# A two-layer transformer encoder: the feed-forward residual loaded in four groups across the output products, and the gate product in the norm's accumulator banks

## The chip, the cores and the metric

One core of one Trainium2 chip runs the whole program. The time is device microseconds (us) of one launch, from the runs' own timer. Engines: TensorE (PE: matmuls; PEld is its weight load), VectorE (DVE), ScalarE (ACT), GpSimd (POOL) and the queues that issue transfers (SPq for SyncE, ACTq for ScalarE). PSUM, the accumulator memory, has 8 banks of 128 x 512 fp32 numbers.

## The reference, cut to what matters

Two layers over 1024 tokens of width 1024. Each layer has a mixer (windowed attention in layer 0, a gated scan in layer 1), a norm, the feed-forward part, a norm, and a gated addition:

```python
x = layer_norm(ALPHA * x + mix, ln_mix_g[i], ln_mix_b[i])
x = layer_norm(ALPHA * x + swiglu(x, ffn_w_in[i], ffn_w_out[i]), ln_ffn_g[i], ln_ffn_b[i])
x = x + jax.nn.sigmoid(x @ ple_w_gate[i]) * (p[i] @ ple_w_proj[i])
```

The change touches the output product of `swiglu` (2816 to 1024), the `ALPHA * x` that is added to it (the residual), the second norm, and the last line's gate product `x @ ple_w_gate[i]`.

## The kernel before, in words

Activations lie transposed, as 8 tiles (128 features x 512 tokens) for each half of the tokens: `Y[m][h]`, m from 0 to 7, h 0 or 1. A product in fp32 is made of three matmuls (`mm3`, L342 to L345) on operands that `split` (L72 to L74) has taken apart into a high part (a copy on ACT) and a low part (a subtraction on DVE or POOL). One such matmul has 128 x 512 outputs.

Everything lives in pools of equal buffers. `A(...)` takes one of 49 SBUF buffers of 128 x 512 fp32 (pool "acts"): raw weights on their way in (`get`, L144 to L147, name `wraw`), the residual `Y`, and most intermediate tiles. `fx["pool"]` (`hp`) has 16 buffers for split operands. PSUM has two pools: `MM(...)` with 3 banks for the whole program, and in this part `bank(...)` with 5 banks (`fps`).

`ffn_ple(li, X, Y, pend)` (L699 to L959) is the feed-forward part of layer `li`; it runs once in each layer. Its stages are `matmuls_in` (22 hidden tiles, L805), `matmuls_out` (L827), and `ple` for each half of the tokens (L918). The output product is made in 7 passes, `ORDER = [1, 2, 6, 7, 4, 5, 3]`, each over 11 steps `k` (FP = 11). A step takes one pair of operands, a weight tile `wo` and a hidden tile `hs`, and adds it into four banks: 12 matmuls. Passes 1, 6, 7 and 4 sum into four banks `ox`, passes 2, 5 and 3 into `oz`, which is one `bank` and three `MM` banks (L877). At the end of a pass, `done(p, i)` (L837 to L863) adds the four results on DVE to four residual tiles: pass 1 uses `Y[0..3][0]` first, pass 6 `Y[0..3][1]`, pass 7 `Y[4..7][1]`, pass 4 `Y[4..7][0]`.

Pairs come through a plan. `take_w("o", p, k, ahead=6)` (L125) hands out the pair of step k, splits pairs until six more are ready, and begins the raw loads of two steps past the last pair split (L115 to L123). Each pair is two loads of 256 KB on SPq, one of `wfo` or its sums and one of the hidden tiles that were kept in memory. The residual is 16 loads of 256 KB on SPq (L834), written ahead of all passes.

When pass 4 is done, the norm of the first half (`norms[0]`) is woven into passes 5 and 3. After pass 3, `weave(ple(0), norms[1], 0.7)` (L954) makes the gate products of the first half (8 products `pgps`, 24 matmuls each) and beside them the norm of the second half: for each step of `ple(0)` (6 matmuls) it takes 0.7 steps of the norm. Products `pgps` are in `MM` banks; the norm's `mu` and `var` (L423, L444) are in `bank`. The gate is read by a sigmoid on ACT (L929), multiplied on DVE (L930) and added to `Y` on POOL (L931). The norm ends, tile by tile, in L452 (DVE), L453 and a copy `xh` (ACT) and `xl` (L74 on POOL); `ple(1)`, the gate products of the second half, reads those.

The kernel writes no order by hand across engines; the instructions of an engine or a queue stand in an order that the building framework makes from the program's order and the buffers that are free. Each engine and queue then works its list from front to end.

Of the kernel before, what the change touches and what calls it, by code (L numbers as in the profile page):

```python
# [17 lines left out]
KT = D // P  # L18
# [9 lines left out]
KH = KT // 2  # L28
# [5 lines left out]
def build(tc, xT, pT, wqkv, watt_o, whg, wvh, whg_o, wfi, wfo, wpg, wpp, sink, lbl, ngd, lnp,  # L34
          rope, amask, hmask, ident, outT):
    nc = tc.nc
    sync, act, dve, pool, pe = nc.sync, nc.scalar, nc.vector, nc.gpsimd, nc.tensor
# [8 lines left out]
    with (  # L46
# [16 lines left out]
        def A(name, dt=F32):  # L63
            return ap_.tile([P, HALF], dt, tag="a", name=name)

        def T(tag, name, bufs=2, dt=F32):
            return tp.tile([P, HALF], dt, tag=tag, bufs=bufs, name=name)

        def MM(name):
            return mp.tile([P, HALF], F32, tag="mm", name=name)  # L70
# [44 lines left out]
        def fetch_w():  # L115
            if at[0] < len(plan):
                while begun[0] < min(at[0] + 3, len(plan)) and (begun[0] <= at[0] or plan[begun[0]][3]):
                    if plan[begun[0]][3]:
                        plan[begun[0]][3]()
                    begun[0] += 1  # L120
                key, fn, args, _ = plan[at[0]]
                ready.append((key, fn(*args)))
                at[0] += 1  # L123

        def take_w(*key, ahead=1):  # L125
            if not ready:
                fetch_w()
            k, w = ready.pop(0)
            assert k == key, (k, key)
            while len(ready) < ahead and at[0] < len(plan) and (not ready or plan[at[0]][3]):  # L130
                fetch_w()
            return w

        fx = {}
# [216 lines left out]
        def lin_steps(w, xs, ps):  # L351
            for k, (wk, xk) in enumerate(zip(w, xs)):
                mm3(ps, wk, xk, k == 0, k == len(xs) - 1)
                if k % 2:
                    yield

        def lin(w, xs, name):
            ps = MM(name)
            yield from lin_steps(w, xs, ps)
            return ps  # L360

        def weave(main, side, ratio=1):
            due = 0.0
            for _ in main:
                due += ratio
                while due >= 1:
                    next(side, None)
                    due -= 1
            drain(side)

        def drain(gen):
            for _ in gen:
                pass
# [6 lines left out]
        def sum_in(s, y, m, yprev, eng=None):  # L380
            if m == 1:
                (eng or dve).tensor_tensor(s, yprev, y, op=ALU.add)
            elif m > 1:
                (dve if m == KT - 1 else eng or dve).tensor_tensor(s, s, y, op=ALU.add)
# [314 lines left out]
        def ffn_ple(li, X, Y, pend):  # L699
            with (  # L700
# [7 lines left out]
                xs = fx["x"] = {p: [] for p in (3, 4, 5, 6, 7)}  # L708
# [5 lines left out]
                def bank(name):  # L714
                    return fps.tile([P, HALF], F32, tag="f", name=name)
# [84 lines left out]
                def store(n=0):  # L800
                    while len(lag) > n:
                        for dst, src in lag.pop(0):
                            act.dma_start(dst, src)
# [22 lines left out]

                def matmuls_out():  # L827
                    s = {}
                    for m in range(KT):
                        for h in range(2):  # L830
                            Y[m][h] = A(f"y{m}{h}")
                    for m0, h in ((0, 0), (0, 1), (KH, 1), (KH, 0)):
                        for m in range(m0, m0 + KH):
                            sync.dma_start(Y[m][h], fx["y"][m, h])  # L834
                    xb, zb = [], []

                    def done(p, i):  # L837
                        x, z = xb[i] if xb else None, zb[i] if zb else None
                        if p == 1:
                            y = Y[i][0]  # L840
                            dve.scalar_tensor_tensor(y, y, ALPHA, x, ALU.mult, ALU.add)
                        elif p == 2:
                            y = Y[i][0]
                            dve.tensor_tensor(y, y, z, op=ALU.add)
                            sum_up(0, i)
                        elif p == 6:
                            y = Y[i][1]
                            dve.scalar_tensor_tensor(y, y, ALPHA, x, ALU.mult, ALU.add)
                        elif p == 7:
                            y = Y[KH + i][1]  # L850
                            dve.scalar_tensor_tensor(y, y, ALPHA, x, ALU.mult, ALU.add)
                        elif p == 4:
                            y = Y[KH + i][0]
                            dve.scalar_tensor_tensor(y, y, ALPHA, x, ALU.mult, ALU.add)
                            sum_up(0, KH + i)
                        elif p == 5:
                            y = Y[KH + i][1]
                            dve.tensor_tensor(y, y, z, op=ALU.add)
                            sum_up(1, KH + i)
                        else:  # L860
                            y = Y[i][1]
                            dve.tensor_tensor(y, y, z, op=ALU.add)
                            sum_up(1, i)  # L863

                    order = {0: list(range(KT)), 1: [*range(KH, KT), *range(KH)]}

                    def sum_up(h, m):
                        n = order[h].index(m)
                        if n == 0:
                            s[h] = T("to", f"s{h}")  # L870
                        sum_in(s[h], Y[m][h], n, Y[order[h][0]][h], pool)

                    for p in ORDER:
                        if p == 1:
                            xb[:] = [bank("ox") for _ in range(4)]
                        elif p in (2, 5):
                            zb[:] = [bank("oz"), *(MM("oz") for _ in range(3))]  # L877
                        into = xb if p in (1, 6, 7, 4) else zb
                        for k in range(FP):
                            if p == 1 and k == 1:  # L880
                                late.pop()()
                            if p == 1 and k == 4:
                                store()
                            w, hh = take_w("o", p, k, ahead=6)
                            for i in range(4):
                                mm3(into[i], w[i], hh, p in (1, 2, 5) and k == 0, k == FP - 1, True)
                                if k == FP - 1:
                                    done(p, i)
                            yield
                            yield  # L890
                        if p == 4:
                            xb.clear()
                            norms[0] = layer_norm([Y[m][0] for m in range(KT)], s[0], li, 1, X, 0, None, bank)
                            yield "half"
                    norms[1] = layer_norm([Y[m][1] for m in range(KT)], s[1], li, 1, X, 1, None, bank)
# [22 lines left out]
                def ple(h):  # L918
                    xs = [X[k][h] for k in range(KT)]
                    for m in range(KT):  # L920
                        pr = T("t1", "pr")
                        sync.dma_start(pr, fx["pr"][m, h])
                        ps = yield from lin(take_w("pg", m, ahead=2), xs, "pgps")
                        sg = T("t0", "psg")
                        end = li == 1 and m == KT - 1
                        w = HALF // 2 if end else HALF
                        for a in range(0, HALF, w):
                            c = slice(a, a + w)
                            act.activation(sg[:, c], ps[:, c], AF.Sigmoid)  # L929
                            dve.tensor_tensor(sg[:, c], sg[:, c], pr[:, c], op=ALU.mult)  # L930
                            (dve if end else pool).tensor_tensor(Y[m][h][:, c], Y[m][h][:, c], sg[:, c], op=ALU.add)  # L931
                            if li == 1:
                                sync.dma_start(outT[m * P:(m + 1) * P, h * HALF + a:h * HALF + a + w], Y[m][h][:, c])
# [6 lines left out]
                norms = {}  # L940
# [10 lines left out]
                while next(out) != "half":  # L951
                    pass
                weave(out, norms[0], 0.9)
                weave(ple(0), norms[1], 0.7)  # L954
                if li == 1:
                    drain(ple(1))
                    return None
# [324 lines left out]
        Y = [[None, None] for _ in range(KT)]  # L1282
# [94 lines left out]
```

## Time and profile before

| | |
|---|---|
| median of 3 runs | 2837.53 us (2830.99 to 2837.82) |
| the profiled execution's own time | 2838.45 us |
| its span, first to last instruction | 2836.7 us |
| mean granted TensorE clock | 0.98 of full speed |
| matmuls | 12852 |
| HBM read, written | 259.84 MB, 88.08 MB |

The span is what the views of the trace are measured in; all stretches are given from its start. A matmul's busy time overlaps the next one's, so that a busy PE is read by how many matmuls start in a stretch. The profile's clock share is 1.00 at 2.4 GHz and 0.50 at 1.2 GHz.

### The profile page before, as it was taken

The page shows a single profiled execution, that of the slowest core. Times are in us where ns is not written, and L with a number is a line of the kernel's source. Part 1 is how long each engine was busy: PE and PEld are TensorE (multiplying, and loading weights), DVE is VectorE, ACT ScalarE, POOL GpSimd, SP SyncE. Part 2 cuts the span into 40 slices and gives each one's busy share as a digit, 9 for nine tenths or more (in the row PEclk, how much of TensorE's full clock was granted, in tenths as well). Part 3 has the DMA queues.
Part 4 walks back from the last instruction along what each step waited for, and adds up shares of the span by engine and source line. Part 5 has one row for each costly group of instructions (what it writes and reads, how often), then busy time and mean ns, then how long its engine had stood idle before and what let it go on. Part 6 is the DMA issues. An engine that isn't in the chain of part 4 may idle for free.

```text
span 2836.7 us, 36978 instructions
## 1 busy us (share of the span) xinstructions
PE 2702.2 (95%) x12852; PEld 2182.9 (77%) x12852; DVE 1840.3 (65%) x2886; ACT 1267.7 (45%) x2482; POOL 1278.8 (45%) x904
## 2 busy tenths in 40 slices
PE   8999999899999899899999999999989999999999
PEld 6666676688888787687878878787667888878777
DVE  6787888755555557827656476667886555556685
ACT  4555667233333445634443344434562333344463
POOL 4233232665565747563222222221336556556563
PEclk9999999999999999999999999999999999999999
DMA  4111136454445952311011111113355444488243
GB/s 164 45 45 45 38 107 220 157 174 151 158 155 180 362 192 92 103 55 54 30 38 34 45 38 34 34 34 125 110 191 195 149 158 147 148 277 301 79 162 112
DMA packets 188827, 350.37 MB, mean 124 GB/s; under 512 B 21472, under 2 KB 24288, under 8 KB 188640
## 3 DMA queue, kind: packets, MB, share of 16 engines
q1 hardware_dynamic: 142560, 264.10, 28.0%
q10 hardware_dynamic: 46080, 83.91, 8.2%
q8 instruction: 101, 1.65, 0.2%
q14 instruction: 86, 0.70, 0.1%
HBM read 259.84 MB, written 88.08 MB: 123 GB/s over the span
## 4 chain that ended last, share of the span: by engine, by line
PE 38%; DVE 7%; POOL 4%; issue 4%; ACT 2%; DMA 1%; SPq 0%; ACTq 0%; POOLq 0%; DVEq 0%
PE zps L345 3%; PE zps L343 3%; PE zps L344 3%; PE lv L1109 3%; PE x L343 3%; PE x L345 3%; PE x L344 3%; POOL wo L74 2%; PE zy L343 1%; PE zy L345 1%; PE zy L344 1%; DVE Q L1079 1%; PE pgps L344 1%; PE pgps L345 1%; PE pgps L343 1%
## 5 line engine op out<-in xcount | busy, mean ns | idle before, releaser
L74 DVE TENSOR_TENSOR wp<-wraw,wp 128x512 fp32r<-128x512 f32 x200 | 212.4, 1063 | 163.2 <-ACT wp L73 135.8
L74 DVE TENSOR_TENSOR hs<-wraw,hs 128x512 fp32r<-128x512 f32 x154 | 208.4, 1371 | 141.9 <-ACT hs L73 139.9
L74 POOL TENSOR_TENSOR wo<-wraw,wo 128x512 fp32r<-128x512 f32 x154 | 225.8, 1479 | 156.8 <-ACT wo L73 155.7
L73 ACT CAST wp<-wraw 128x512 fp32r<-128x512 f32 x200 | 124.6, 623 | 294.1 <-PE x L345 149.5
L74 POOL TENSOR_TENSOR w_hz<-r_hz,w_hz 128x512 fp32r<-128x512 f32 x70 | 96.1, 1379 | 301.1 <-ACT w_hz L73 292.9
L343 PE MATMUL x<-xc,wp 128*128 128x512 f32 x528 | 211.2, 401 | 10.3 <-ACT u L728 7.2
L345 PE MATMUL x<-xc,wp 128*128 128x512 f32 x528 | 210.9, 399 | 0.0
L344 PE MATMUL x<-xc,wp 128*128 128x512 f32 x528 | 210.1, 398 | 0.0
L343 PE MATMUL zps<-xh_n,w_hz 128*128 128x512 f32 x512 | 209.9, 410 | 0.0
L345 PE MATMUL zps<-xh_n,w_hz 128*128 128x512 f32 x512 | 203.6, 398 | 0.9 <-POOL w_hz L74 0.9
L344 PE MATMUL zps<-xl_n,w_hz 128*128 128x512 f32 x512 | 202.8, 396 | 0.0
L73 ACT CAST wo<-wraw 128x512 fp32r<-128x512 f32 x154 | 95.4, 620 | 190.0 <-POOL wo L74 114.4
L343 PE MATMUL ox<-hs,wo 128*128 128x512 f32 x352 | 137.9, 395 | 11.4 <-ACT hs L73 11.4
L345 PE MATMUL ox<-hs,wo 128*128 128x512 f32 x352 | 139.1, 395 | 1.3 <-POOL wo L74 1.3
L344 PE MATMUL ox<-hs,wo 128*128 128x512 f32 x352 | 139.5, 396 | 0.4 <-DVE hs L74 0.3
L186 POOL TENSOR_TENSOR wraw<-s,wraw 128x512 f32<-128x512 f32 x34 | 45.1, 1325 | 202.5 <-DVE wp L74 201.7
L343 PEld LDWEIGHTS x<-xc,wp 128*128 128x128 f32 x528 | 100.0, 189 | 37.4 <-ACT u L728 8.1
L345 PEld LDWEIGHTS x<-xc,wp 128*128 128x128 f32 x528 | 100.0, 189 | 25.4 <-DVE wp L74 0.6
L344 PEld LDWEIGHTS x<-xc,wp 128*128 128x128 f32 x528 | 100.0, 189 | 23.5
L345 PEld LDWEIGHTS zps<-xh_n,w_hz 128*128 128x128 f32 x512 | 97.4, 190 | 21.4 <-POOL w_hz L74 1.3
L344 PEld LDWEIGHTS zps<-xl_n,w_hz 128*128 128x128 f32 x512 | 97.7, 191 | 16.7
L343 PEld LDWEIGHTS zps<-xh_n,w_hz 128*128 128x128 f32 x512 | 97.5, 190 | 16.3
(380 smaller groups left out, 8197.1 us busy)
## 6 DMA issues: line engine op xcount, KB each, us to landing
wraw<-in_wfi_dram SPq DMA_DIRECT2D x196, 256.0 KB, 3.2
wraw<-in_wfo_dram SPq DMA_DIRECT2D x154, 256.0 KB, 4.1
wraw<-h SPq DMA_DIRECT2D x154, 256.0 KB, 4.9
wraw<-w SPq DMA_DIRECT2D x88, 256.0 KB, 5.3
r_hz<-in_whg_dram SPq DMA_DIRECT2D x70, 256.0 KB, 2.8
w<-wraw ACTq DMA_DIRECT2D x66, 256.0 KB, 2.9
h<-th ACTq DMA_DIRECT2D x66, 256.0 KB, 2.1
r_pg<-in_wpg_dram SPq DMA_DIRECT2D x32, 512.0 KB, 4.2
```

The source lines that it names most:

```text
L73: act.copy(hi, src)
L74: (eng or dve).tensor_tensor(lo, src, f32(hi), op=ALU.subtract)
L186: pool.tensor_tensor(a11, tmp, a11, op=ALU.subtract)
L343: pe.matmul(ps, lhsT=w[0], rhs=x[0], start=start, stop=False, skip_group_check=free)
L344: pe.matmul(ps, lhsT=w[0], rhs=x[1], start=False, stop=False, skip_group_check=free)
L345: pe.matmul(ps, lhsT=w[1], rhs=x[0], start=False, stop=stop, skip_group_check=free)
L1079: dve.tensor_tensor(Qq[:, 1 - d], qk[:, 0], t["F"][:, d], op=ALU.mult)
L1109: pe.matmul(lv[:, c], lhsT=ks[:, c * P:(c + 1) * P], rhs=view(Qq, c * P, dims), start=True, stop=True)
```

## The change

`lin` takes a bank from its caller if one is given. The 16 residual loads are no longer written ahead of the passes, but in four groups of four, at steps k = 5 to 8 of passes 1, 2, 6 and 7: each ahead of that step's `take_w`, each with its own buffer taken at that point. The gate products take a `bank` in place of an `MM` bank, and the weave of the gate products with the second norm takes 0.85 steps of the norm for a step in place of 0.7.

```diff
-        def lin(w, xs, name):
-            ps = MM(name)
+        def lin(w, xs, name, ps=None):
+            ps = MM(name) if ps is None else ps
...
                 def matmuls_out():
                     s = {}
-                    for m in range(KT):
-                        for h in range(2):
-                            Y[m][h] = A(f"y{m}{h}")
-                    for m0, h in ((0, 0), (0, 1), (KH, 1), (KH, 0)):
-                        for m in range(m0, m0 + KH):
-                            sync.dma_start(Y[m][h], fx["y"][m, h])
+                    wanted = {p: [(m0 + i, h) for i in range(KH)]
+                              for p, m0, h in ((1, 0, 0), (2, 0, 1), (6, KH, 1), (7, KH, 0))}
...
                             if p == 1 and k == 4:
                                 store()
+                            if p in wanted and k >= 5 and wanted[p]:
+                                m, h = wanted[p].pop(0)
+                                Y[m][h] = A(f"y{m}{h}")
+                                sync.dma_start(Y[m][h], fx["y"][m, h])
                             w, hh = take_w("o", p, k, ahead=6)
...
-                        ps = yield from lin(take_w("pg", m, ahead=2), xs, "pgps")
+                        ps = yield from lin(take_w("pg", m, ahead=2), xs, "pgps", bank("pgps"))
...
-                weave(ple(0), norms[1], 0.7)
+                weave(ple(0), norms[1], 0.85)
```

## Rows read from the trace of the kernel before

**Rows 1.** The page: busy us (share of the span) x instructions, by engine.

```profile
PE 2702.2 (95%) x12852; PEld 2182.9 (77%) x12852; DVE 1840.3 (65%) x2886; ACT 1267.7 (45%) x2482; POOL 1278.8 (45%) x904
```

**Rows 2.** Waits of PE over the span: us in total, times, longest.

```profile
PE ox L343 <- ACT hs L73: 11.4, 2, 8.4
PE pgps L343 <- DVE y L862: 6.0, 2, 4.3
PE pgps L344 <- POOL xl L74: 4.4, 6, 1.1
```

**Rows 3.** Layer 0's pass 1 in stretches: PE, PEld, DVE, ACT, POOL busy (x); clock; DMA share, GB/s.

```profile
925.00:930.00 5.00, 0.76 (x4) 0.30 (x2) 0.00 (x0) 0.00 (x0) 0.00 (x0) 1.00 0.83 281
930.00:935.00 5.00, 0.80 (x2) 0.71 (x3) 0.82 (x1) 1.85 (x3) 1.45 (x2) 0.51 1.02 362
935.00:940.00 5.00, 5.00 (x13) 3.83 (x13) 1.22 (x2) 1.14 (x2) 4.92 (x4) 0.50 1.05 391
...
950.00:980.00 30.00, 30.00 (x134) 24.86 (x133) 25.60 (x21) 18.20 (x32) 24.77 (x17) 1.00 1.05 386
```

**Rows 4.** Timeline of SPq, layer 0, then layer 1: start, us, what.

```profile
901.58 0.33 SPq L79 DMA_DIRECT2D r_hv<-in_wvh_dram  x1
...
912.93 15.34 SPq L834 DMA_DIRECT2D y<-y  x16
928.37 0.38 SPq L146 DMA_DIRECT2D wraw<-in_wfo_dram  x1
...
2509.59 12.85 SPq L834 DMA_DIRECT2D y<-y  x16
```

**Rows 5.** Timeline of ACT, then POOL, layer 0's pass 1: [idle before <- releaser].

```profile
932.86 0.62 ACT L73 CAST wo<-wraw 128x512 fp32r<-128x512 f32 x1 [15.08 <-DMA wraw<-in_wfo_dram]
...
941.24 0.62 ACT L73 CAST hs<-wraw 128x512 fp32r<-128x512 f32 x1 [3.20 <-POOL th L789]
...
919.40 1.74 POOL L74 TENSOR_TENSOR w_hz<-r_hz,w_hz 128x512 fp32r<-128x512 f32 x1
```

**Rows 6.** Matmuls into `ox` in two stretches: us, PE busy (x), PEld, DVE, clock, DMA.

```profile
910.16:951.75 41.59, 32.52 (x128) 25.72 (x127) 1.07 (x2) 0.88 0.89 309
2511.16:2547.29 36.13, 32.05 (x128) 24.69 (x127) 0.67 (x1) 0.95 0.94 320
```

**Rows 7.** The page's DMA issues (median us to landing), and `done` of passes 7 and 4 by tile.

```profile
y<-y SPq DMA_DIRECT2D x32, 256.0 KB, 4.5
...
L851 DVE SCALAR_TENSOR_TENSOR y<-y,ox x8: 673/674/687, 1039.9 to 2638.4; 128x512 f32<-128x512 f32 x8
L854 DVE SCALAR_TENSOR_TENSOR y<-y,ox x8: 673/674/689, 1070.0 to 2668.5; 128x512 f32<-128x512 f32 x8
```

**Rows 8.** Timeline from pass 3 to `ple(0)`: PE in both layers, DVE and ACT in layer 0.

```profile
1142.59 0.77 PE L343 MATMUL pgps<-xh,w_pg 128*128 128x512 f32 x1 [4.33 <-DVE y L862]
...
2737.33 0.47 PE L343 MATMUL pgps<-xh,w_pg 128*128 128x512 f32 x1 [1.72 <-DVE y L862]
...
1147.11 0.68 DVE L384 TENSOR_TENSOR s<-s,y 128x512 f32<-128x512 f32 x1
...
1151.16 0.60 ACT L929 ACTIVATE psg<-pgps 128x512 f32<-128x512 f32 x1 [1.16 <-PE pgps L345]
1151.65 0.61 ACT L73 CAST avh<-s 128x512 fp32r<-128x512 f32 x1
```

**Rows 9.** Matmuls into `pgps` in stretches (PE, PEld, ACT); POOL at the end of the norm.

```profile
1142.59:1151.16 8.57, 8.57 (x25) 6.83 (x26) 0.00 (x1) 0.65 0.07 22
...
1195.00:1207.00 12.00, 9.42 (x27) 6.60 (x26) 0.60 (x1) 0.72 0.30 108
1207.00:1219.00 12.00, 12.00 (x53) 9.66 (x52) 1.20 (x2) 1.00 0.16 44
...
2787.00:2793.00 6.00, 4.20 (x16) 2.50 (x15) 0.00 (x0) 1.00 0.57 197
...
1195.45 5.07 POOL L74 TENSOR_TENSOR xl<-y,xh 128x512 fp32r<-128x512 f32 x3
```

## The prediction

> **What bounds the kernel now.** I read the page first: TensorE is busy 95% of the span, no other engine over 77% [rows 1]. So time is won only where TensorE stands still or runs at half clock. The waits of PE name three such places in this part of the program, once in each layer: the output product waits for a hidden tile's copy (11.4 us), the first gate product waits for the DVE instruction that reads the last `oz` (6.0), and the second half's gate products wait for `xl`, the norm's last tiles (4.4) [rows 2]. The idle time is not all of it, so I took stretches next. In layer 0, TensorE starts 2 matmuls from 930 to 935 us and 13 from 935 to 940, at a clock share of 0.51 and 0.50, that is 1.2 GHz, after five microseconds in which it was almost idle; from 950 to 980 it starts 134 at 2.4 GHz [rows 3]. A normal pass takes 30.1 us (`done` of pass 7 at 1039.9, of pass 4 at 1070.0) for 132 matmuls, 0.228 us each [rows 7]. The first pass's 128 uninterrupted matmuls into `ox` took 41.59 us in layer 0 and 36.13 in layer 1, where 128 x 0.228 = 29.2 would do [rows 6]: 12.4 and 6.9 us are lost.
>
> The queue shows why. All 16 residual loads go out in a row, from 912.93 for 15.34 us; the weight for step 6 follows at 928.37 [rows 4], and ACT, which has to copy it, has waited 15.08 us for it when it starts at 932.86 [rows 5]. Layer 1 has the same 16 in 12.85 us [rows 4]. The first residual tile is not read before the end of the pass.
>
> **The residual loads.** Without them the load for step 6 can go out at 912.93, 15.4 us earlier. With the 4.5 us to landing of such a load [rows 7] its ACT copy can start at 917.4. TensorE wants the pair after 68 of the 128 matmuls, at 910.16 + 68 x 0.228 = 925.7. POOL is held by a hoisted split of the next stage until 919.40 + 1.74 = 921.1 [rows 5], so the low part of `wo` comes at about 922.6: three microseconds in hand. The two pairs behind came slowly before: the copy of the third `hs` started at 941.24, 8.4 us after the first `wo` copy, since ACT's list has stores in it that wait for POOL's `th` [rows 5]. Moved forward, the third pair is whole at 921.1 + 8.4 + 1.4 for copy and subtraction = 930.9, against 925.7 + 2 x 2.74 = 931.2 wanted. That is so near that I take 0.8 us of loss in layer 0, and none in layer 1, where that hoisted split is absent. Ends: 0 (the copies become the next stall) and 12.4 + 6.9; I take 11.6 + 6.9 = **18.5 us**, near the upper end, because the queue's 15.34 us is the row that fits the idle time.
>
> The loads don't vanish. By the code, when step 5's residual load is written, the loads up to step 12 have been begun; six pairs are on their way at 912.93, so 14 loads stand ahead of the first residual. At the 0.96 us that one of the 16 took [rows 4] it goes out at 926.3, the fourth, nine loads later, at 934.9, and lands at 939.4. The pass then ends at 910.16 + 29.2 = 939.4: just in time. If a tile is late, DVE's `done` waits, and behind it on DVE stand the `hs` subtractions of later pairs; six split pairs are in hand, 72 x 0.228 = 16.4 us, before TensorE notices. The other three groups are loaded one pass (30.1 us) before they are read. The loads cost the 16 issues they always cost, beside a TensorE that needs one pair, 512 KB, in 2.74 us (191 GB/s) where the transfers run at 386 GB/s [rows 3]. So nothing, with that cover.
>
> The Trainium skill (Trainium Kernel Development and Optimization, Key Constraints) says that the transfers of all queues run on the same 16 engines and interleave. By that, moving loads makes no room: if transfers bound this stretch, the stall would only move; this is the second rival.
>
> **The gate product's bank.** `oz` fills one `bank` and three `MM` banks, so the first `pgps` in `MM` waits until DVE has read the second `oz`: idle 4.33 us in layer 0, 1.72 in layer 1 [rows 8]. In layer 0 the next 25 matmuls then take 8.57 us at a clock share of 0.65 [rows 9], in place of 5.7. Together 7.2 and 1.7 us. In `bank` the four `ox` banks have long been read, and the product can start at once; the price is that `mu` and `var` need two of the five, which leaves three, as many as `MM` had, so I see no loss from it. At `ple(1)` TensorE waits for `xl`: 27 matmuls start in 12 us where 53 do in the next 12, 26 x 0.226 = 5.9 us lost; in layer 1, 16 start in 6 us instead of 26.5, 2.4 lost [rows 9]. Upper end of this part 7.2 + 5.9 + 1.7 + 2.4 = 17.2; lower end 0, if the norm's end doesn't move, for then TensorE only waits longer at `ple(1)`.
>
> How far does the norm's end move? Its sum is ready at 1147.11 + 0.68 = 1147.8, but ACT copies it (`avh`) at 1151.65, because the sigmoid of product 0 stands ahead and waits for TensorE [rows 8]. With product 0 done 7.2 us sooner the copy is bound by the sum: 3.6 us gained (51.65 - 48.0). In layer 1 I take 0.5, between 0 and 1.7. The ratio: the norm's 22 steps now need 22/0.7 = 31.4 of the 32 steps of `ple(0)`, then 22/0.85 = 25.9; 5.5 steps x 6 x 0.228 = 7.5 us earlier in the program's order. POOL ends the norm with `xl` at 1.7 us each [rows 9], work that doesn't shrink, so I take half, 3.8. The norm's end moves 7.4 us in layer 0, TensorE's arrival 7.2: the wait stays, gain 7.4. In layer 1, 4.3 against 1.7: the wait goes, gain 1.7 + 2.4 = 4.1. Together **11.5 us**.
>
> The Trainium skill (TensorE: Matmul & The Clock Gate, HAM oscillation) reports a kernel in which PSUM double-buffering gave no further gain. By that this part would bring 0. The trace speaks against it here, with 4.33 us of idle time that ends on the read of a bank; still it is the first rival's outcome.
>
> Sum: 18.5 + 11.5 = 30.0 us. Against the profiled execution's 2838.45 us (span 2836.7 and 1.75 around it), which lies 0.9 above the median, that gives 2808.4; I say 2808. The scan behind layer 0 should pass its share on, since TensorE is the bound there too.
>
> **The rivals.** *The norm decides.* TensorE starts `ple(0)` earlier and waits as much longer for `xl`; only the first part counts: 2838.45 - 18.5 = 2820. For it: POOL's `xl` follow each other without a gap [rows 9]. Against: ACT's `avh` hung on TensorE. 0.20. *Transfers bind.* From 950 to 980 us they are at a share of 1.05 [rows 3]. Then the eight residual loads of passes 1 and 2 come back as waits, 8 x 0.96 = 7.7 us a layer: 2808.4 + 15.4 = 2824. Against: pairs need half the rate. 0.10. *The order doesn't follow the program.* The trace has a load of the next stage on the queue at 901.58, ahead of this stage's [rows 4]; if free buffers again pull the residual loads to the front, and the norm's end moves only 3.6 + 0.5, the time is 2834. 0.09. *Slower.* A residual load that waits for a buffer blocks all weights behind it on SPq, at the end of pass 1 in both layers. It decides from 16.4 us of lateness on; to lose some 20 us in each layer beyond the 30.0 gained, a tile must land a whole pass late, and then it is 2838.45 - 30.0 + 40 = 2848. Nothing in the queue's rows is that late. 0.06.
>
> **How the numbers follow.** The forecast case has the remaining 0.55. The range 2796 to 2827 goes from all upper ends (12.4 + 6.9 + 17.2 = 36.5, that is 2802, less about 6 for the spread of the runs, 2831 to 2838) to the transfer rival with 3 for the spread; it leaves out the last two rivals, 0.15. A measurement can tell about 0.3%, 8.5 us. Faster by more: 0.55 + 0.20 + 0.10 = 0.85; within: 0.09; slower: 0.06.
>
> **What would show it.** Right: no 15 us row of `y` on SPq; 128 `ox` matmuls in 29 to 31 us in both layers, at 2.4 GHz; four `y` loads between 920 and 940; no PE wait of `pgps` on `y` L862; `avh` at about 1.5 us after the last `oz` sum. Wrong: a PE wait on `hs` or `wo` later in pass 1 or 2, a DVE wait of L841 on a transfer, or a longer wait of `pgps` on `xl`.

## The result and the profile after

The changed kernel takes 2801.32 us (median of 4 runs, 2800.38 to 2803.96). The kernel before, run beside it, takes 2834.26 us (2830.77 to 2837.82). The ratio is 0.9883 with a 95% interval of 0.9871 to 0.9895: 32.9 us less, where 30.0 was forecast. The profiled execution of the changed kernel has 2800.78 us and a span of 2799.0 us.

TensorE's busy time falls from the 2702.2 us of [rows 1], mostly because fewer of its matmuls run at half clock (some 55 fewer over the span, at about 0.2 us each). The other engines do what they did. From the page:

```profile
PE 2685.0 (96%) x12852; PEld 2174.8 (78%) x12852; DVE 1844.1 (66%) x2886; ACT 1265.4 (45%) x2482; POOL 1281.2 (46%) x904
```

The waits of PE (us in total, times, longest). All three of [rows 2] are gone, the one on `hs` and both of `pgps`. Of the output product's first pass there is one wait of 0.2 us left, the last line; `mu`, the norm's average, waits for `avh` at two places more than before (4.8 us in 4 waits).

```profile
PE mu L389 <- ACT avh L73: 4.8, 4, 1.4
PE oz L343 <- DVE y L854: 4.3, 2, 2.2
...
PE ox L345 <- POOL wo L74: 0.2, 1, 0.2
```

**Pass 1.** The 128 matmuls of [rows 6], as stretches of the changed kernel in layer 0 and layer 1 (us, PE, PEld and DVE busy with their counts, clock, DMA share, GB/s). They take 29.57 and 29.04 us instead of 41.59 and 36.13, at a clock of 1.00: 12.0 and 7.1 us less.

```profile
907.33:936.90 29.57, 29.37 (x128) 23.77 (x127) 0.00 (x0) 1.00 0.83 275
2483.91:2512.95 29.04, 29.04 (x128) 23.86 (x127) 0.00 (x0) 1.00 0.93 329
```

The timeline of SPq in layer 0 (start, us, what) has no row of 15 us as in [rows 4]. The four residual loads stand among the pairs, one for each step. The weight for step 6, which went out at 928.37 behind the row, goes out at 910.13: 2.8 us after the first of the 128 matmuls starts, in place of 18.2.

```profile
910.13 0.41 SPq L146 DMA_DIRECT2D wraw<-in_wfo_dram  x1
...
929.94 0.33 SPq L146 DMA_DIRECT2D wraw<-h  x1
930.31 0.87 SPq L883 DMA_DIRECT2D y<-y  x1
931.24 0.42 SPq L146 DMA_DIRECT2D wraw<-in_wfo_dram  x1
931.71 0.43 SPq L146 DMA_DIRECT2D wraw<-h  x1
932.18 0.43 SPq L883 DMA_DIRECT2D y<-y  x1
...
935.38 0.43 SPq L883 DMA_DIRECT2D y<-y  x1
```

The pass ends at 936.90. DVE's first use of a residual tile comes 7.8 us behind that, and TensorE shows no wait for it. DVE did not wait for the tile either: it came from `hs` subtractions that stand ahead in its list and that wait for ACT's copies (timeline of DVE; no idle time before the last line):

```profile
943.49 1.24 DVE L74 TENSOR_TENSOR hs<-wraw,hs 128x512 fp32r<-128x512 f32 x1 [0.47 <-ACT hs L73]
944.65 0.68 DVE L837 SCALAR_TENSOR_TENSOR y<-y,ox 128x512 f32<-128x512 f32 x1
```

**The gate products.** PE, DVE and ACT in layer 0, from three timelines, the places of [rows 8]. The last `oz` matmul starts at 1124.88, the first `pgps` 0.23 us later. ACT copies the sum (`avh`) as soon as DVE has it, ahead of the first sigmoid (L929), and now it is `mu` that waits:

```profile
1125.11 0.40 PE L343 MATMUL pgps<-xh,w_pg 128*128 128x512 f32 x1
...
1130.51 0.68 DVE L384 TENSOR_TENSOR s<-s,y 128x512 f32<-128x512 f32 x1
...
1131.22 0.62 ACT L73 CAST avh<-s 128x512 fp32r<-128x512 f32 x1 [1.16 <-DVE s L384]
...
1131.89 0.50 PE L389 MATMUL mu<-avh,ones 128*128 128x512 f32 x1 [1.02 <-ACT avh L73]
```

The end of the norm on POOL in layer 0: six `xl` in one row, one addition to `Y` (L931), then the last two. The last `xl` is done at 1176.29, 51.4 us behind the last `oz` matmul; TensorE waits for none of them.

```profile
1159.25 1.67 POOL L931 TENSOR_TENSOR y<-y,psg 128x512 f32<-128x512 f32 x1 [5.75 <-DVE psg L930]
1160.89 10.28 POOL L74 TENSOR_TENSOR xl<-y,xh 128x512 fp32r<-128x512 f32 x6
1171.13 1.75 POOL L931 TENSOR_TENSOR y<-y,psg 128x512 f32<-128x512 f32 x1
1172.85 3.44 POOL L74 TENSOR_TENSOR xl<-y,xh 128x512 fp32r<-128x512 f32 x2
```

**The account.** Of the 37.7 us between the two spans (2836.7 and 2799.0), pass 1 has 12.0 + 7.1. The stretch from the first `oz` matmul of pass 2 to the last `pgps` matmul has 10.3 in layer 0 (951.75 to 1242.81, now 936.90 to 1217.67) and 3.3 in layer 1 (2547.29 to 2831.38, now 2512.95 to 2793.70). The other 5.0 us lie where nothing was changed: 2.8 ahead of pass 1 of layer 0, 2.1 between the two layers' stretches.

### The profile page after: what moved, and what is told of

It is laid out like the page before. It is cut to its first block, busy times and chain, and to the rows that moved or that the text cites. A ratio compares the mean times of both kernels' runs of the same rounds, so it can differ in the third digit from the quotient of the medians.

```text
span 2799.0 us, 36983 instructions
## 1 busy us (share of the span) xinstructions
PE 2685.0 (96%) x12852; PEld 2174.8 (78%) x12852; DVE 1844.1 (66%) x2886; ACT 1265.4 (45%) x2482; POOL 1281.2 (46%) x904
## 4 chain that ended last, share of the span: by engine, by line
PE 68%; DVE 11%; issue 6%; POOL 5%; ACT 5%; DMA 4%; ACTq 0%; SPq 0%; POOLq 0%; DVEq 0%
PE x L343 5%; PE x L345 5%; PE x L344 5%; PE zps L345 3%; PE zps L343 3%; PE zps L344 3%; PE lv L1109 3%; PE zy L343 3%; PE zy L345 3%; PE zy L344 3%; POOL wo L74 2%; PE s L560 2%; PE pgps L345 2%; PE pgps L344 2%; PE pgps L343 2%
## 5 line engine op out<-in xcount | busy, mean ns | idle before, releaser
L74 POOL TENSOR_TENSOR w_hz<-r_hz,w_hz 128x512 fp32r<-128x512 f32 x70 | 96.4, 1383 | 298.7 <-ACT w_hz L73 290.5
L343 PE MATMUL x<-xc,wp 128*128 128x512 f32 x528 | 211.6, 402 | 11.5 <-ACT u L728 8.4
```

Of the source, the lines that this page charges most:

```text
L74: (eng or dve).tensor_tensor(lo, src, f32(hi), op=ALU.subtract)
L343: pe.matmul(ps, lhsT=w[0], rhs=x[0], start=start, stop=False, skip_group_check=free)
```

## The experiments

The two parts were first taken apart. For each kernel the table gives its time, the time of pass 1's 128 matmuls, and the stretch just named, which holds all that the second part can touch. A stretch is read from the starts of PE's matmuls: a normal step is 0.228 us, a step at half clock 0.43. "Half" is the number of half-clock steps, "waits" what the longer steps have above 0.228 us, in us. Every stretch here comes out within 0.5 of 271.8 us plus these two losses (a half-clock step loses 0.2 us). Each cell is layer 0 / layer 1.

| kernel | median us | pass 1 | stretch | half | waits |
|---|---|---|---|---|---|
| before, profiled execution | 2838.45 (one) | 41.6 / 36.1 | 291.1 / 284.1 | 32 / 8 | 12.9 / 10.5 |
| before, another execution | 2829.60 (one) | 42.0 / 36.3 | 284.9 / 284.1 | 7 / 8 | 11.3 / 10.5 |
| four groups alone | 2812.06 | 29.5 / 29.0 | 286.4 / 285.6 | 15 / 16 | 11.4 / 10.6 |
| groups and bank, ratio 0.7 | 2810.98 | 29.6 / 29.0 | 284.3 / 283.7 | 8 / 8 | 10.6 / 9.8 |
| groups and ratio 0.85, MM bank | 2802.52 | 29.6 / 29.0 | 280.7 / 281.3 | 8 / 6 | 7.3 / 8.6 |
| bank and ratio 0.85 alone | 2821.52 | 42.9 / 36.5 | 280.7 / 280.7 | 8 / 8 | 7.4 / 7.4 |
| the change | 2801.32 | 29.6 / 29.0 | 280.8 / 280.8 | 8 / 7 | 7.4 / 7.4 |

### The residual groups alone

```diff
-                        ps = yield from lin(take_w("pg", m, ahead=2), xs, "pgps", bank("pgps"))
+                        ps = yield from lin(take_w("pg", m, ahead=2), xs, "pgps")
-                weave(ple(0), norms[1], 0.85)
+                weave(ple(0), norms[1], 0.7)
```

> The residual in four groups; gate product back in an MM bank, ratio back at 0.7. Theory (the 16 loads stood ahead of the seventh pair on the queue, and the two parts add): 18.5 to 19.0 us below the kernel before (11.6 to 12.0 in layer 0, 6.9 to 7.0 in layer 1), so about 2815.5; the waits of the gate product on y L862 and on xl are those of before (6.0 and 4.4 us). Rival (the parts need each other, because what pass 1 gains is waited off at the norm): less than 12 us below before, with longer waits on xl. Rival (the gain of this part is all there is): 33 us below, as the whole change.

2812.06 us against 2835.99 of the kernel before (ratio 0.992, 0.9905 to 0.9934). Pass 1 takes 29.52 and 29.04 us: the whole gain of 12.1 and 7.1 us comes from this part alone. The 23.9 us are more than that. In the trace the waits for `xl` are those of before, 4.4 us; the waits on the MM bank came to 6.9. The stretch of layer 0 took 286.4 us instead of 291.1 mainly because 15 matmuls instead of 32 ran at half clock. The rival in which the gain is waited off at the norm falls, and so does the one in which this part is all there is.

### The bank and the ratio alone

```diff
-                    wanted = {p: [(m0 + i, h) for i in range(KH)]
-                              for p, m0, h in ((1, 0, 0), (2, 0, 1), (6, KH, 1), (7, KH, 0))}
+                    for m in range(KT):
+                        for h in range(2):
+                            Y[m][h] = A(f"y{m}{h}")
+                    for m0, h in ((0, 0), (0, 1), (KH, 1), (KH, 0)):
+                        for m in range(m0, m0 + KH):
+                            sync.dma_start(Y[m][h], fx["y"][m, h])
```

> The 16 residual loads ahead of all passes as before; bank and ratio 0.85 as in the change. Theory: the gate stage keeps its own gain, 10.5 us in layer 0 and 3.4 in layer 1, so 11.5 (predicted) to 14 us below the kernel before, about 2821; pass 1 still has its 11.4 us of wait on hs and its half clock. Rival (the norm decides, the wait on xl only grows): 0 to 4 us below before. Rival (order: the five banks of the norm and the output product were freed early only because pass 1 ended earlier): below 8 us.

2821.52 us against 2835.99 (ratio 0.9945, 0.9928 to 0.9961): 14.5 us. The stretch is 280.7 us in both layers, the same as with the whole change, and pass 1 still loses what it lost before (42.9 and 36.5 us). So the parts do not need each other, and all three rivals fall. The medians give 23.9 + 14.5 = 38.4 for the parts and 32.9 for both; with intervals of 3 to 5 us to either side of each, that is no sign that they don't add. In the traces they do: pass 1 takes with the groups alone what it takes with the whole change, and the stretch does so with the bank and the ratio alone.

### The bank without the ratio, and the ratio without the bank

```diff
-                weave(ple(0), norms[1], 0.85)
+                weave(ple(0), norms[1], 0.7)
```

> Groups and bank as in the change, ratio back at 0.7. Predicted share of the ratio: 3.8 us in layer 0, so with the bank alone the norm's end moves only about 3.6 us against 7.2 of TensorE: 3 to 4 us above the changed kernel, with the waits on xl back and longer than the 4.4 us of before (the xl copies again split by L931). Rival (the bank does it all, the ratio is idle): within 1 us of the changed kernel, no wait on xl. Rival (the ratio is the main thing): 7 us or more above.

```diff
-                        ps = yield from lin(take_w("pg", m, ahead=2), xs, "pgps", bank("pgps"))
+                        ps = yield from lin(take_w("pg", m, ahead=2), xs, "pgps")
```

> Groups and ratio 0.85 as in the change, gate product back in an MM bank. Theory: the wait on y L862 is back, 4.3 us in layer 0 and 1.7 in layer 1, and with it half-clock matmuls worth 2.9 us in layer 0; the later avh then gives back another 0 to 3 us as waits on xl: 6 to 12 us above the changed kernel. Rival (the bank wait is absorbed because the norm comes earlier by the ratio): 0 to 3 us above. Rival (the half clock was chance): 6 us above, with the clock at 1.00 in the 9 us behind the wait.

Without the ratio the time is 2810.98 us (ratio 0.9912, 0.9898 to 0.9927), 1.1 us below the groups alone. Without the bank it is 2802.52 (0.9882, 0.9868 to 0.9897), 1.2 us above the whole change, which is within the spread. The theory was wrong in both: the first comes out as the rival said in which the ratio is the main thing (9.7 us above the change), the second as the rival in which the bank wait is absorbed. By the stretches, the ratio is worth 5.7 + 4.3 us where the bank is absent and 3.5 + 3.0 where it is there; the bank is worth 2.1 + 1.9 at a ratio of 0.7, and -0.1 + 0.6 at 0.85. Part of this is half clock, which differs between executions; by the waits alone the ratio is worth 4.1 + 2.0 and 3.2 + 2.4 us, the bank 0.8 + 0.8 and -0.1 + 1.2.

Why the bank brings nothing at 0.85 is seen in the waits of PE with the ratio alone. The wait on `y` is back, and the two new ones on `mu` are gone: TensorE waits for the same stretch of DVE's list, in one place or the other.

```profile
PE pgps L343 <- DVE y L858: 3.0, 2, 2.3
PE mu L389 <- ACT avh L73: 2.8, 2, 1.4
```

Why the ratio brings so much is seen on POOL. With the bank and a ratio of 0.7, layer 0 (the last `oz` matmul starts at 1126.16):

```profile
1161.29 1.67 POOL L931 TENSOR_TENSOR y<-y,psg 128x512 f32<-128x512 f32 x1 [5.85 <-DVE psg L930]
1164.96 3.24 POOL L74 TENSOR_TENSOR xl<-y,xh 128x512 fp32r<-128x512 f32 x2 [1.99 <-ACT xh L73]
1168.82 1.68 POOL L931 TENSOR_TENSOR y<-y,psg 128x512 f32<-128x512 f32 x1 [0.63 <-DVE psg L930]
1170.46 5.17 POOL L74 TENSOR_TENSOR xl<-y,xh 128x512 fp32r<-128x512 f32 x3
1176.26 1.68 POOL L931 TENSOR_TENSOR y<-y,psg 128x512 f32<-128x512 f32 x1 [0.62 <-DVE psg L930]
1177.90 5.07 POOL L74 TENSOR_TENSOR xl<-y,xh 128x512 fp32r<-128x512 f32 x3
```

Between the `xl` stand two additions of 1.7 us, each of which has waited for a gate product's sigmoid and multiplication, and the first `xl` has waited 1.99 us for `xh` on ACT. The last `xl` ends at 1182.97, 56.8 us behind the last `oz` matmul, against 51.4 at a ratio of 0.85.

### Where the ratio's gain comes from: position or pace

My explanation at this point was that ACT's `avh` stands behind the sigmoid of product 0 at a ratio of 0.7 and ahead of it at 0.85: by the code the average is the third step of the norm, which falls on the fifth step of the gate products (0.7 x 5 = 3.5) or on the fourth (0.85 x 4 = 3.4). Two kernels move it ahead with a slow norm; a third makes the norm faster still.

```diff
-                weave(ple(0), norms[1], 0.85)
+                next(norms[1])
+                weave(ple(0), norms[1], 0.7)
```

> Ratio 0.7 as before, but one step of the second norm ahead of the gate products, so that its average is written before the sigmoid of product 0; groups and bank as in the change. Theory (the gain of the ratio is in two parts: avh ahead of the first sigmoid on ACT, 1.7 to 2.0 us, and the additions to Y no longer between the low parts xl on POOL, 3.6 us): from the last oz matmul to the last pgps matmul 94 to 95.5 us in both layers, against 96 with the bank alone and 92.8 in the changed kernel, some waits on xl left. Rival (position of avh is all): 92.8, no wait on xl. Rival (pace is all): 96, as with the bank alone.

```diff
-                weave(ple(0), norms[1], 0.85)
+                weave(ple(0), norms[1], 0.76)
```

> The change with a ratio of 0.76: the average of the second norm is still written ahead of the sigmoid of product 0 (its third step falls on the fourth step of the gate products, as at 0.85), but the norm's last tiles come later, with an addition to Y after four xl and one after three. Theory (what counts is where the average stands against the sigmoid, and that no more than one addition stands between the xl that TensorE needs next): mu and avh as in the changed kernel, the last xl 1.7 to 3 us later against 1.6 us of slack, so from the last oz to the last pgps matmul 92.8 to 94.5 us, 0 to 3 us above the changed kernel. Rival (pace is all): halfway between 0.7 and 0.85, 94.5 us a layer and 3 to 5 us above. Rival (position is all): 92.8 and 0.

```diff
-                weave(ple(0), norms[1], 0.85)
+                weave(ple(0), norms[1], 1.0)
```

> The change with a ratio of 1.0: mu moves one step of six matmuls ahead, in front of six matmuls that TensorE could have done while DVE ends the sum. Theory: no xl wait is left to win at 0.85, and mu now waits 1.4 us longer for avh (2.4 in place of 1.0), with half-clock matmuls behind it in some layer: 1 to 5 us above the changed kernel. Rival (the earlier norm still gains): 0 to 3 us below.

| kernel | median us (ratio to before, interval) | stretch | half | waits |
|---|---|---|---|---|
| one step ahead, 0.7 | 2814.07 (0.9925, 0.9910 to 0.9940) | 287.3 / 287.0 | 24 / 24 | 10.7 / 10.3 |
| ratio 0.76 | 2809.97 (0.9907, 0.9892 to 0.9922) | 284.4 / 283.9 | 8 / 8 | 10.9 / 10.3 |
| ratio 1.0 | 2814.66 (0.9921, 0.9905 to 0.9936) | 288.0 / 288.1 | 21 / 18 | 12.2 / 13.0 |

From the last `oz` to the last `pgps` matmul, ratio 0.76 takes 96.4 and 95.9 us where 92.8 to 94.5 was expected, as much as 0.7 with the bank (96.4 and 95.7). So it is neither of the two rivals' numbers, and the explanation falls: with `avh` where the changed kernel has it, nothing is gained. POOL at 0.76 in layer 0 (last `oz` matmul 1126.57) points to the order at the norm's other end:

```profile
1164.75 6.64 POOL L74 TENSOR_TENSOR xl<-y,xh 128x512 fp32r<-128x512 f32 x4 [1.99 <-ACT xh L73]
1173.23 1.71 POOL L931 TENSOR_TENSOR y<-y,psg 128x512 f32<-128x512 f32 x1 [1.83 <-DVE psg L930]
1174.90 5.14 POOL L74 TENSOR_TENSOR xl<-y,xh 128x512 fp32r<-128x512 f32 x3
1180.00 1.73 POOL L931 TENSOR_TENSOR y<-y,psg 128x512 f32<-128x512 f32 x1
1181.69 1.71 POOL L74 TENSOR_TENSOR xl<-y,xh 128x512 fp32r<-128x512 f32 x1
```

The first `xl` waits 1.99 us again. POOL then stands 1.83 us idle for a gate product, with two finished `xh` behind it in its list, and a third by its end. The last `xl` ends at 1183.40, 56.8 us behind the last `oz` matmul, just as at 0.7. Against the changed kernel's 51.4 the first `xl` starts 2.2 us later behind the last `oz` (38.2 and 36.0), and the idle time and a second addition bring 3.5 more. So the 5.4 us are accounted for, but no run changes POOL's order by itself: how much of the gain is the order and how much the earlier norm is not shown.

The other side of the optimum costs as much. With one step ahead, and with 1.0, `mu` moves in front of six matmuls that TensorE could have done, and waits 1.96 us for `avh` in layer 0 instead of 1.02. At 1.0 the norm's `var` waits as well, 2.57 us in layer 0. Neither kernel gains, and both lie above everything that was expected (99.3 and 99.0 us from the last `oz` to the last `pgps` for the one, 100.1 and 101.7 for the other). Both have 18 to 24 half-clock steps, which is half of the loss against the changed kernel for the one (3.2 of 6.5 us in layer 0) and a third for the other (2.6 of 7.2); the rest are waits.

### The place of the residual loads

```diff
-                            if p in wanted and k >= 5 and wanted[p]:
-                                m, h = wanted[p].pop(0)
-                                Y[m][h] = A(f"y{m}{h}")
-                                sync.dma_start(Y[m][h], fx["y"][m, h])
+                            if p == 1 and k == 5:
+                                for m0, h in ((0, 0), (0, 1), (KH, 1), (KH, 0)):
+                                    for m in range(m0, m0 + KH):
+                                        Y[m][h] = A(f"y{m}{h}")
+                                        sync.dma_start(Y[m][h], fx["y"][m, h])
```

> All 16 residual loads in one row at step 5 of pass 1, the rest as in the change. Theory (a row of 15 us on the one queue delays whatever stands behind it, and six split pairs cover it): the row goes out at about 930 us in layer 0, so the loads of the pair 14 places behind the queue's front go out at about 945; the pairs in hand last 16.4 us, so the loss is 0 to 5 us a layer, time 0 to 8 us above the changed kernel, with a wait of oz or ox on an operand early in pass 2 and none in pass 1. Rival (it is enough to load late, grouping is idle): 0, no such wait. Rival (transfers bind): 6 us a layer or more.

```diff
+                    for m in range(KH):
+                        Y[m][0] = A(f"y{m}0")
+                        sync.dma_start(Y[m][0], fx["y"][m, 0])
                     wanted = {p: [(m0 + i, h) for i in range(KH)]
-                              for p, m0, h in ((1, 0, 0), (2, 0, 1), (6, KH, 1), (7, KH, 0))}
+                              for p, m0, h in ((2, 0, 1), (6, KH, 1), (7, KH, 0))}
```

> The first four residual loads ahead of all passes, the other twelve in their groups. Theory (TensorE's wait is the time of the row of loads, less what the split pairs hold): four loads of 0.96 us put the seventh pair 3.8 us later, against 3 us in hand in layer 0: 0 to 2 us above the changed kernel, pass 1 in layer 0 at 36 to 38 us, in layer 1 at 35.5. Rival (any residual load ahead of the passes costs its share, 4 of 16): 3.0 us in layer 0 and 1.8 in layer 1. Rival (copies, not loads, pace pass 1): 0 and unchanged waits.

All 16 in one row at step 5: 2812.54 us (ratio 0.992, 0.9905 to 0.9934), 11.2 us above the changed kernel. The row goes out where expected, in 10.02 us instead of 15, and TensorE stands still as soon as the pairs in hand are used up, early in pass 2 (SPq, then PE, layer 0):

```profile
929.98 10.02 SPq L882 DMA_DIRECT2D y<-y  x16
940.43 0.33 SPq L146 DMA_DIRECT2D wraw<-in_wfo_dram  x1
...
947.18 0.53 PE L343 MATMUL oz<-hs,wo 128*128 128x512 f32 x1 [4.59 <-ACT hs L73]
948.44 0.80 PE L344 MATMUL oz<-hs,wo 128*128 128x512 f32 x1 [0.72 <-DVE hs L74]
```

These two steps are 5.8 us above normal ones, and the 12 half-clock matmuls behind them cost 2.4 us: 8.2 us in layer 0, above the 5 us that were the upper bound even without the half clock. The cover there was less than the 16.4 us of the expectation: the row began 12.4 us before TensorE wanted the first pair behind it, and TensorE could start on that pair only 17.2 us after the row's start. In layer 1 the row has 9.88 us but began 18.5 us ahead (2510.38, for a pair wanted at 2528.8), and no such wait follows. Some 3 us of the 11.2 lie elsewhere: `mu` waits 2.67 and 2.66 us in place of 1.02 and 1.00, and the rest is not explained. The rival that late is enough falls. The one that the transfers bind, at 6 us in each layer, falls with layer 1; whether in layer 0 the queue's order or the full transfer engines (a DMA share of 1.06 in the 7 us of the wait) held the pair back is not told apart, since a row of loads fills both. All 16 also take their buffers at once here, which no run tests by itself.

Four ahead, twelve in groups: 2805.34 us (ratio 0.9898, 0.9882 to 0.9915). The four go out in 4.66 us, and pass 1 takes 30.61 us in layer 0 and 29.04 in layer 1, that is 1.0 us and 0.0 above the change. The seventh pair had some 3 us in hand, and only what exceeds that is paid; a price by shares (3.0 and 1.8) and none at all are both excluded. The median's 4.0 us above the changed kernel, measured in another set of runs, lies within the two intervals; the profiled execution has 2801.04. What the other part is stays open.

### Two attempts to do better

```diff
-                weave(out, norms[0], 0.9)
+                weave(out, norms[0], 0.75)
```

> The change with the first norm woven at 0.75 in place of 0.9 into passes 5 and 3. Theory (the 2.2 us in which pass 3 waits for DVE's read of pass 5's sums comes from norm steps ahead of that read): this wait goes in both layers, 1.8 us each, part of it given back as a longer wait of mu on avh: 0 to 4 us below the changed kernel. Rival (DVE paces the end of pass 3 in any order, so that the wait moves to mu): 0. Rival (the first norm now ends too late for the first gate product): 2 to 6 us above, with waits of pgps on xl.

```diff
-                        def fin(box=box):
+                        def fin(box=box, early=h == 0 and m < 3):
...
-                                split(hl[:, 0], hl[:, 1], box[0][:, c])
+                                split(hl[:, 0], hl[:, 1], box[0][:, c], pool if early and c else None)
```

> The change with three subtractions w_pg of the first gate products on POOL, in its 5.9 us of idle time ahead of the last sums, in place of DVE. Theory (DVE's row of w_pg subtractions ahead of its last reads of oz holds the sum up): avh 1 to 3 us earlier, the 1.0 us waits of mu on avh gone: 1 to 3 us below the changed kernel. Rival (ACT's copies w_pg or TensorE hold the sum up): 0. Rival (DVE and POOL slow each other, or POOL's sums come later): 0 to 3 above.

The slower first norm gives 2807.93 us (ratio 0.9908, 0.9893 to 0.9922), 6.6 us above the changed kernel. `oz` waits 2.57 us for DVE instead of 2.17, and `mu` then 4.28 instead of 1.02, with the clock at 0.62 in the 8 us behind it: the sum comes 8.9 us behind the last `oz` matmul (1122.99 to 1131.87) instead of 5.6. The wait on `oz` was to go and did not. The second mechanism had the wait move to `mu`, but at no cost; the third had the size, by waits of `pgps` on `xl`, and there are none. Three subtractions on POOL give 2812.11 us (0.9918, 0.9901 to 0.9934). ACT, DVE and POOL in layer 0, from three timelines:

```profile
1118.50 1.15 ACT L73 CAST w_pg<-r_pg 128x512 fp32r<-128x512 f32 x2 [8.73 <-POOL w_pg L74]
...
1119.15 0.69 DVE L74 TENSOR_TENSOR w_pg<-r_pg,w_pg 128x512 fp32r<-128x512 f32 x1 [6.82 <-ACT w_pg L73]
...
1117.18 1.28 POOL L74 TENSOR_TENSOR w_pg<-r_pg,w_pg 128x512 fp32r<-128x512 f32 x1
```

POOL came to its first of them at 1117.18, behind its `xl` and `wo`. ACT's next copy waited 8.73 us for that, DVE 6.82 us for ACT, and `mu` 6.46 us in layer 0. The loss, 10.8 us against the change, is more than any side had said. POOL's idle time lay behind the place where the work was needed. No version tried here beats the changed kernel.

### The kernel before once more

> The kernel before once more, for the spread of one stage between executions. If the half clock of layer 0's gate stage (0.65 behind the wait of 4.3 us, 0.72 among the waits on xl) belongs to the kernel, the stage from the last oz to the last pgps matmul takes 104.9 us in layer 0 and 96.2 in layer 1 again, within 0.5; if it is chance, layer 0 comes out at 100 to 103. The first pass of the output product should take 48.1 and 42.6 us again.

Pass 1's 128 matmuls take 41.99 and 36.31 us, close to the 41.59 and 36.13 of [rows 6]. The gate stage of layer 0, from the last `oz` to the last `pgps` matmul, takes 97.0 us and not 104.9, lower still than the 100 to 103 said for chance, and close to layer 1 (96.2). The waits of PE, and the two stretches that answer to [rows 9] (us, PE, PEld and ACT busy with their counts, clock, DMA share, GB/s):

```profile
PE pgps L344 <- POOL xl L74: 4.4, 6, 1.2
...
PE pgps L343 <- DVE y L862: 3.5, 2, 1.7
```

```profile
1137.49:1146.10 8.61, 8.61 (x36) 6.80 (x37) 0.60 (x1) 1.00 0.31 107
1187.40:1199.40 12.00, 9.39 (x38) 6.71 (x37) 0.81 (x2) 1.00 0.29 105
```

In the same 12 us with the same waits for `xl`, 38 matmuls start here at a clock of 1.00, and 27 at 0.72 in [rows 9]. So the half clock in layer 0's gate stage is not in every execution of the kernel. How often it comes is not shown; the medians of the kernel before (2834 to 2838) lie between these two executions (2838.45 and 2829.60). The second part of the change is worth 10.3 us in layer 0 against the execution that I predicted from, and 4.2 against this one.

## Why the prediction was right, and where it was wrong

**The residual loads: right, in place and size.** 11.6 + 6.9 was predicted; 12.0 + 7.1 was measured, with the groups alone as with the whole change. The step "the copies become the next stall" was priced at 0.8 us in layer 0; 0.2 us of it is to be seen. The place of the row was the cause, and not the bytes: four loads ahead cost 1.0 us, and 16 in a row at step 5 cost 8.2 in layer 0 and nothing in layer 1, while the same 16 in groups cost nothing.

What the row's 15.34 us are made of, the prediction did not ask. "0.96 us that one of the 16 took" is no time of a load: one issue takes 0.3 to 0.5 us, and for half of the two rows (14 of 28.2 us) the queue stood until an earlier transfer had landed, most of all stores of the stage before on ACT's queue (SPq's waits in the kernel before, both rows together: us in total, times, longest):

```profile
SPq L834 <- DMA h<-h: 6.0, 2, 4.3
SPq L834 <- DMA w<-wraw: 5.3, 3, 2.4
SPq L834 <- DMA h<-g: 1.5, 2, 1.2
```

The changed kernel's queue meets such waits among its weights: one of 5.2 us on a store holds an `h` load back until 929.94. By then the weight for step 6 has long gone out, and TensorE shows no wait. At step 5, behind most of those stores, the row took 10.0 us and not 15.

"Just in time" was not tested. The first residual load went out at 930.31 where 926.3 was worked out, the fourth at 935.38 (934.9), and it landed at 941.4, 4.5 us behind the end of the pass; DVE reached the first tile only at 944.65, for a reason of its own. How much of the 16.4 us of split pairs that needed is not shown.

**The bank and the ratio: the sum was near by luck, its terms were wrong.** 11.5 us was predicted, 13.6 measured against the profiled execution, 7.5 against the other one. The bank was priced too high and the ratio too low, and the two errors cancel. Four steps failed:

- "Together 7.2 and 1.7 us" for the bank in layer 0 was read from a wait of 4.33 us and the half clock behind it. In the other execution that wait is 1.72 us with the clock at 1.00, and with the groups alone it is 3.44 in both layers at 0.80. A term that rested on one execution was taken as the kernel's.
- "TensorE's arrival 7.2" would be a gain if nothing else waited for DVE there. The read of `oz`, the norm's sum and `avh` are one stretch of DVE's list. At 0.85 TensorE, let through at the first gate product, stands at `mu` instead (1.02 us in layer 0, 1.00 in layer 1), and the bank is worth -0.1 and 0.6 us. The prediction set the Trainium skill (TensorE: Matmul & The Clock Gate, HAM oscillation) against this step, with its kernel that gained nothing from PSUM double-buffering; for the bank at a ratio of 0.85 the measurement is on its side.
- "the copy is bound by the sum: 3.6 us gained" rested on the same execution, in which `avh` starts 13.8 us behind the last `oz` matmul. In the other it starts 8.5 us behind, and with the bank at a ratio of 0.7 8.1: 0.4 gained. Nor does an earlier `avh` by itself move the norm's end: with 0.76 and with one step ahead it starts 6.3 us behind, and the last `xl` ends 56.8 and 58.2 us behind, in place of 56.8.
- "Work that doesn't shrink, so I take half, 3.8" for the ratio. The `xl` themselves took the 1.7 us each that was assumed. What shrank is what stood among them on POOL, additions to `Y` that wait for gate products, and the wait for the first `xh`. The last `xl` came 5.4 us earlier (56.8 to 51.4 us behind the last `oz`), enough for "the wait stays" in layer 0 to be false. The ratio is the main term of this part: 3.5 + 3.0 us with the bank, 5.7 + 4.3 without it.

**The rivals.** "The norm decides" (2820) is what came out with the ratio undone, but at 2811: the bank did little and the waits for `xl` stayed. "Transfers bind" falls with the stretches behind the first group of residual loads in layer 0 (us, PE busy, clock, DMA share, GB/s): the transfers are full, and TensorE starts as many matmuls as it can.

```profile
935.00:945.00 10.00, 10.00 (x46) 1.00 1.03 377
945.00:955.00 10.00, 10.00 (x46) 1.00 1.05 386
```
The order did follow the program. The slower case, a residual load that waits for a buffer and holds up the weights, was not seen. What holds them up is a load that waits for an earlier transfer, as in the row of the kernel before, or the row itself, as at step 5. In groups of four neither reached TensorE.

**The size.** 2808 was forecast for a measured 2801.3. Against the profiled execution the change brought 19.1 + 13.6 where 18.5 + 11.5 was said. The remaining 5.0 us of the difference come from parts of the program that weren't touched and vary between executions: the kernel before, executed again, has only 1.6 us of it (2.8 becomes -1.9 ahead of pass 1 of layer 0, 2.1 becomes 3.5 between the two layers' stretches).

## What to carry to other kernels

A row of loads that nobody needs yet, written ahead of loads that are needed soon, can cost up to the length of the row, less the time by which the first operands behind it would have been early: 12.0 and 7.1 us here for rows of 15.34 and 12.85, and nothing where a row of 9.88 began 18.5 us ahead. Read too what the row itself waits for. Put each load a little ahead of its use, among the loads that are needed sooner. When a wait is taken away, look at who else waits for the same engine's list: here the bank only moved TensorE's wait from the gate product to `mu`. And before a stage is priced, look at the same stage in the other layer or in another execution: half-clock stretches come and go, and 5 us of this forecast hung on them.

## What the runs showed that was not expected

The same kernel in the same stretch had 32 half-clock matmuls in one execution and 7 in another, and the other kernels had 6 to 26. Waits of equal length do not settle it. Behind the 2.17 us wait on `oz`, the changed kernel ran 8 matmuls at half clock in layer 0 and 7 in layer 1; with the ratio alone, the same wait of 2.17 us in layer 1 was followed by none. Longer waits do not settle it either. The clock share was 0.80 in the 8.6 us behind a wait of 3.44 us, 0.65 behind 4.33 and 0.62 in the 8 us behind 4.28, but behind the two waits of 2.57 us on `oz` with the slower first norm it stayed at 1.00. The Trainium skill (TensorE: Matmul & The Clock Gate, The HAM clock gate) says of the number of matmuls at the lower clock at a kernel's start that it is "run-variable"; these traces show the same in the middle of one, 7 against 32. Which idle time will be followed by it is left open here.

The norm's ratio has a narrow optimum, 0.85 among the four values tried. 0.7 and 0.76 leave the stretch some 3 us longer in each layer, as long as each other, and 1.0 makes it 7 us longer.
